# Norm tiles in the two banks of a PSUM pair declared independent of each other, reads by VectorE and ScalarE included

## The chip, the cores and the metric

The kernel runs on one core of a Trainium2 chip, in one launch. The metric is device time in microseconds (us), the median of three runs.

## The reference, cut to what matters

Two layers of a diffusion backbone run over 512 latent tokens (stream X) and 256 context tokens (stream C), model width 1024, in float32. Each sublayer is wrapped in two RMS norms ("sandwich"): the input of a sublayer is normed and modulated, its output is normed, scaled by a gate and added to the stream.

```
xm = rmsnorm(h, g_in) * (1 + scale) + shift          # "pre"
y  = sublayer(xm)                                     # SwiGLU, conv + Fourier mixer, or attention
h  = h + gate * rmsnorm(y, g_out)                     # "post"
```

The sublayers are SwiGLU, conv + Fourier mixer, SwiGLU in layer 0, and SwiGLU, attention, SwiGLU in layer 1. Five times a post of one sublayer is followed by the pre of the next, for each stream; the last post has no pre behind it.

## The kernel before, in words

Tokens lie along the free dimension and the 1024 features along 128 partitions in KT = 8 tiles. Every matrix product is done in three passes: operands are split in a high and a low part, and `mm3` (lines 209 to 216) issues `w_high x_high`, `w_high x_low`, `w_low x_high`. So each feature tile k of a normed input has a high part, made by ScalarE, and a low part, made by VectorE, and the second of three matmuls needs the low part.

`run` (line 107) walks a list of items, each some weight chunks and a function that issues the matmuls. Raw weights come in by SP's queue, ScalarE rounds them to `wh` (line 141), VectorE or GpSimd makes `wl` (line 143); while a norm is under way (`self.norms`) it is always GpSimd. Norms are generators that `advance` steps while matmuls are issued, by a clock that counts TensorE time; `yield 1.8` means that 1.8 us of matmuls are issued before the next piece. The framework then plans the order of each engine's queue from priorities and modelled durations, and puts in semaphore waits for the dependencies that it tracks on tiles.

A norm of one stream goes: `rnorm` (line 254) sums squares over partitions on TensorE (L261), makes a reciprocal root on VectorE (L279 to L288), and spreads it on TensorE (L267). Then `post` (line 319) does per tile k, all on VectorE unless said: a scaled `y` into PSUM scratch `t` (L331, "post norm"), the previous tile's addition of squares (L245), `h += t` (L335), and on ScalarE the square of `h` into `t` (L244). `pre` and `pre_tiles` (lines 291 to 318) do per tile: scaled `h` into scratch `t` (L311, "norm"), on ScalarE `x_high = t + B` (L313, "high"), and on VectorE `x_low = (t + B) - x_high` (L304, "low"). The order written is norm(k), high(k), low(k-1).

`scratch` (line 225) gives `t`. Streams of lane "c" (C, and B, the second half of the last sublayer) get a `mm` tile of their own, one bank, three in rotation. Streams of lane "x" (X with 512 columns, and A, the first half, with 256) get a half of a `pr` tile of 1024 columns, which spans two banks: even k the first half, odd k the second. In `pre` all eight tiles alternate in one `pr`; in `post` each pair k, k+1 takes a new `pr`, of two.

After the pre of X TensorE runs `lead4`, `lead6` or the latent projections: it goes through k = 0 to 7 with six matmuls of 512 columns (256 for A) per tile, and so consumes normed tiles as they come.

Of the kernel before, what the change touches and what calls it, by code (L numbers as in the profile page):

```python
# [10 lines left out]
F32 = mybir.dt.float32  # L11
# [3 lines left out]
AF = mybir.ActivationFunctionType  # L15
ALU = mybir.AluOpType
# [60 lines left out]
class Builder:  # L77
# [158 lines left out]
    def stats_add(self, s, st, src, sq, late=False):  # L236


        nc = self.nc
        if st.ssum is None:  # L240
            st.ssum = self.tmp.tile([P, s.n], F32, name=self.nm("ssum"), tag=f"ssum{s.lane}", bufs=1)
            nc.scalar.activation(out=st.ssum, in_=src, func=AF.Square)
        else:
            nc.scalar.activation(out=sq, in_=src, func=AF.Square)  # L244
            add = lambda: nc.vector.tensor_tensor(out=st.ssum, in0=st.ssum, in1=sq, op=ALU.add)  # L245
            if late:
                return add
            add()

    def new_stats(self):  # L250
# [47 lines left out]
    def pre_tiles(self, s, ks, A, B, rb):  # L298

        nc = self.nc  # L300
        done, last = [], None

        def low(k, x, t):
            nc.vector.scalar_tensor_tensor(out=x[:, 1], in0=t, scalar=B[:, k:k + 1], in1=x[:, 0].bitcast(F32),  # L304
                                           op0=ALU.add, op1=ALU.subtract)
            done.append((x[:, 0], x[:, 1]))

        for k in ks:
            x = self.xmpool.tile([P, 2, s.n], F32R, name=self.nm("xm"), tag=f"xm{s.name}{k}", bufs=1)
            t = self.scratch(s, k, True)  # L310
            nc.vector.scalar_tensor_tensor(out=t, in0=s.h[k], scalar=A[:, k:k + 1], in1=rb,  # L311
                                           op0=ALU.mult, op1=ALU.mult)
            nc.scalar.activation(out=x[:, 0], in_=t, func=AF.Identity, bias=B[:, k:k + 1])  # L313
            if last:
                low(*last)
            last = k, x, t
        low(*last)
        return done

    def post(self, s, st, A, want_stats=True):  # L320

        nc = self.nc
        y = s.y
        yield N1 if s.lane != "c" else N1C
        rb = yield from self.rnorm(s, st, D)
        new = self.new_stats()
        late = None
        for k in range(KT):
            with self.tc.high_priority(PRIORITY):
                t = self.scratch(s, k)  # L330
                nc.vector.scalar_tensor_tensor(out=t, in0=y[k], scalar=A[:, k:k + 1], in1=rb,  # L331
                                               op0=ALU.mult, op1=ALU.mult)
                if late:
                    late()
                nc.vector.tensor_tensor(out=s.h[k], in0=s.h[k], in1=t, op=ALU.add)  # L335
                if want_stats:
                    late = self.stats_add(s, new, s.h[k], t, True)
                    if k == KT - 1:
                        late()
            yield POST[0] if s.n == 512 else POST[1]  # L340
        yield 2.0
        return new
# [828 lines left out]
    def attend(self, gaps):  # L1171

        heads = [(g, kind, hd) for g in range(4) for kind, hd in HEADS]
        st, loads, wts = {}, {}, {}
        soft, avs, post, ends = [], [], [], []

        gap = 1.0
# [479 lines left out]
```

## Time and profile before

| | |
|---|---|
| runs | 2997.32, 2997.54, 2999.41 us; median 2997.54 |
| profiled execution | 2996.09 us, of which the span of instructions is 2994.3 us |
| mean granted TensorE clock | 0.988 |
| busy share of the span | TensorE 96%, VectorE 55%, ScalarE 35%, GpSimd 27% |
| DMA | 413 MB, mean 138 GB/s |

TensorE is busy nearly all the time, so what counts are the short stretches in which it waits, and the stretches in which its clock is granted at half. Busy shares of the other engines are averages over stages and tell little about such a stretch; the timelines of the stretch do. The five stretches in which a pre of lane "x" feeds TensorE begin at about 607, 850, 1431, 2010 and 2600 us of the span; they are called S1 to S5 here. S1 is the mixer's input, S2 and S3 the inputs of the two SwiGLUs behind it, S4 that of attention, S5 that of the last SwiGLU (stream A).

### The profile page before, as it was taken

The numbers are of one execution on the slowest core, as the hardware profiler recorded it, in microseconds if no ns is written. First come the engines' busy times: TensorE is split into PE (matmuls) and PEld (weight loads), VectorE is DVE, ScalarE is ACT, GpSimd is POOL, SyncE is SP. The second block draws the span as 40 slices with busy tenths as digits, with TensorE's granted clock in tenths as the row PEclk, the third lists the DMA queues.
The fourth block names the chain that finished last, engine by engine and source line by source line (L and its number), as shares of the span: only waits on it lengthen the run. The fifth ranks groups of instructions, "written<-read, shape, count | busy, mean of one in ns | idle before, by whom it ended". The sixth has DMA issues, their size and how long they took to land.

```text
span 2994.3 us, 44211 instructions
## 1 busy us (share of the span) xinstructions
PE 2874.3 (96%) x17842; PEld 2549.9 (85%) x17842; DVE 1650.9 (55%) x2966; ACT 1043.5 (35%) x1733; POOL 820.5 (27%) x441
## 2 busy tenths in 40 slices
PE   6999999999999999999999999999899999999998
PEld 5888888878878888888788888887788888899997
DVE  7866676565475433435845334366366667653335
ACT  4422121444343221124431122244344555552223
POOL 4221112423242111114311111143433332442222
PEclk9999999999999999999999999999999999999999
DMA  7754433323344322233333433352866685452334
GB/s 269 248 166 134 141 135 127 120 86 126 120 142 148 112 85 99 78 120 113 124 130 106 131 116 118 108 167 100 265 166 185 154 211 111 146 175 92 102 103 141
DMA packets 190095, 413.19 MB, mean 138 GB/s; under 512 B 58369, under 2 KB 83585, under 8 KB 189890
## 3 DMA queue, kind: packets, MB, share of 16 engines
q1 hardware_dynamic: 126930, 373.09, 37.6%
q0 software_dynamic: 62960, 37.27, 5.6%
q8 instruction: 140, 2.29, 0.3%
q14 instruction: 65, 0.53, 0.1%
HBM read 375.14 MB, written 35.00 MB: 137 GB/s over the span
## 4 chain that ended last, share of the span: by engine, by line
PE 63%; DVE 6%; DMA 3%; issue 2%; ACT 2%; POOL 2%; SPq 0%; ACTq 0%; POOLq 0%; DVEq 0%
PE mm L213 12%; PE mm L215 12%; PE mm L214 12%; PE pr L214 8%; PE pr L213 8%; PE pr L215 8%; PE pr L1021 2%; PE mm L1030 1%; ACT wh L141 1%; DVE wl L143 1%; DMA ks<-dr 1%; PE st L1115 1%; POOL wl L143 1%; DVE top L1011 1%; DMA dr<-stg 1%
## 5 line engine op out<-in xcount | busy, mean ns | idle before, releaser
L143 POOL TENSOR_TENSOR wl<-wraw,wh 128x1024 fp32r<-128x1024 f32 (+2 forms) x276 | 674.8, 2448 | 1898.1 <-ACT wh L141 1887.5
L141 ACT ACTIVATE wh<-wraw 128x1024 fp32r<-128x1024 f32 (+1 forms) x476 | 494.2, 1039 | 940.7 <-PE mm L214 577.8
L214 PE MATMUL pr<-xm,wh 128*128 128x512 f32 (+1 forms) x1760 | 635.5, 361 | 22.9 <-DVE xm L304 18.1
L213 PE MATMUL pr<-xm,wh 128*128 128x512 f32 (+1 forms) x1760 | 632.3, 360 | 8.3 <-DVE act L221 2.9
L215 PE MATMUL pr<-xm,wl 128*128 128x512 f32 (+1 forms) x1760 | 632.3, 359 | 0.0
L213 PE MATMUL mm<-xm,wh 128*128 128x256 f32 (+1 forms) x1560 | 460.1, 296 | 8.0 <-DVE xm L304 5.0
L215 PE MATMUL mm<-xm,wl 128*128 128x256 f32 (+1 forms) x1560 | 461.5, 296 | 1.8 <-DVE wl L143 1.8
L214 PE MATMUL mm<-xm,wh 128*128 128x256 f32 (+1 forms) x1560 | 460.4, 295 | 0.6 <-DVE xm L304 0.6
L213 PE MATMUL mm<-act,wh 128*128 128x256 f32 (+1 forms) x1408 | 454.1, 324 | 5.9 <-ACT y L504 2.1
L215 PE MATMUL mm<-act,wl 128*128 128x256 f32 (+1 forms) x1408 | 454.0, 323 | 2.6 <-POOL wl L143 2.6
L214 PE MATMUL mm<-act,wh 128*128 128x256 f32 (+1 forms) x1408 | 454.1, 323 | 1.5 <-DVE act L221 1.5
L214 PEld LDWEIGHTS pr<-xm,wh 128*128 128x128 f32 x1760 | 334.6, 190 | 83.5 <-DVE xm L304 27.0
L383 DVE CUSTOM_DVE_ANT_0 junk<-wmod,cond,bmod 128x1024 bf16<-128x1024 f32 x256 | 387.8, 1515 | 9.6 <-DMA wmod<-in_w_mod_dram 6.9
L213 PEld LDWEIGHTS pr<-xm,wh 128*128 128x128 f32 x1760 | 334.5, 190 | 61.4 <-DVE act L221 3.3
L215 PEld LDWEIGHTS pr<-xm,wl 128*128 128x128 f32 x1760 | 334.9, 190 | 51.2
L143 DVE TENSOR_TENSOR wl<-wraw,wh 128x1024 fp32r<-128x1024 f32 x200 | 251.5, 1257 | 210.0 <-ACT wh L141 209.5
L213 PEld LDWEIGHTS mm<-xm,wh 128*128 128x128 f32 x1560 | 295.7, 190 | 18.3 <-DVE xm L304 5.6
L215 PEld LDWEIGHTS mm<-xm,wl 128*128 128x128 f32 x1560 | 295.3, 189 | 10.2 <-DVE wl L143 2.4
L214 PEld LDWEIGHTS mm<-xm,wh 128*128 128x128 f32 x1560 | 295.3, 189 | 8.8 <-DVE xm L304 1.1
L213 PEld LDWEIGHTS mm<-act,wh 128*128 128x128 f32 x1408 | 265.3, 189 | 33.1 <-ACT act L220 3.6
L214 PEld LDWEIGHTS mm<-act,wh 128*128 128x128 f32 x1408 | 266.6, 189 | 26.2 <-DVE act L221 2.7
L215 PEld LDWEIGHTS mm<-act,wl 128*128 128x128 f32 x1408 | 265.8, 189 | 26.8 <-POOL wl L143 3.2
(240 smaller groups left out, 3445.7 us busy)
## 6 DMA issues: line engine op xcount, KB each, us to landing
wraw<-in_w_ffn_in_dram SPq DMA_DIRECT2D x250, 512.0 KB, 3.5
wmod<-in_w_mod_dram SPq DMA_DIRECT2D x160, 512.0 KB, 4.3
wraw<-in_w_ffn_out_dram SPq DMA_DIRECT2D x106, 512.0 KB, 3.6
dr<-stg SPq DMA_DIRECT2D x40, 512.0 KB, 4.7
wraw<-in_w_in_even_dram SPq DMA_DIRECT2D x32, 512.0 KB, 3.5
qs<-dr POOLq DMA_DIRECT2D x56, 256.0 KB, 11.7
dr<-stg SPq DMA_DIRECT2D x36, 256.0 KB, 6.7
ks<-dr POOLq DMA_DIRECT2D x24, 384.0 KB, 11.2
```

The source lines that it names most:

```text
L141: self.nc.scalar.activation(out=h, in_=r, func=AF.Copy)
L143: eng.tensor_tensor(out=l, in0=r, in1=h.bitcast(F32), op=ALU.subtract)
L213: mmul(out, w[0], x[0], start=first, stop=False)
L214: mmul(out, w[0], x[1], start=False, stop=False)
L215: mmul(out, w[1], x[0], start=False, stop=last)
L383: dot = nc.vector.tensor_tensor_reduce(out=junk, in0=w, in1=self.cond[n], op0=ALU.mult, op1=ALU.add, scale=1.0, scalar=self.bmod[:, l, row ...
L1011: nc.vector.tensor_reduce(top, ps, axis=AX.X, op=ALU.max, negate=True)
L1021: self.nc.tensor.matmul(ps[:, c0:c1], q, k[:, c0:c1], start=i == 0, stop=i == len(passes) - 1)
L1030: self.nc.tensor.transpose(ps[:, kt * P:(kt + 1) * P], w[:, (k0 + kt) * P:(k0 + kt + 1) * P], self.ident)
L1115: nc.tensor.matmul(ps, v[:, kt], wt[i][:, :, kt], start=kt == 0 and i == 0, stop=kt == 5 and i == 1)
```

## The change

The tiles' tracker treats accesses to one `pr` tile as dependent; the change declares certain pairs of instructions, which touch different halves, to be without dependency. In `pre_tiles`, for lane "x": norm(k+1) on high(k), and low(k) on high(k+1). In `post`, for lane "x" and odd k: post norm(k) on the square of k-1. `stats_add` returns the square's instruction for that. No instruction is added, removed or rewritten.

```diff
-            nc.scalar.activation(out=st.ssum, in_=src, func=AF.Square)
+            return nc.scalar.activation(out=st.ssum, in_=src, func=AF.Square), None
         else:
-            nc.scalar.activation(out=sq, in_=src, func=AF.Square)
+            square = nc.scalar.activation(out=sq, in_=src, func=AF.Square)
...
-                return add
+                return square, add
...
-        def low(k, x, t):
-            nc.vector.scalar_tensor_tensor(out=x[:, 1], in0=t, scalar=B[:, k:k + 1], in1=x[:, 0].bitcast(F32),
-                                           op0=ALU.add, op1=ALU.subtract)
+        def low(k, x, t, other=None):
+            ins = nc.vector.scalar_tensor_tensor(out=x[:, 1], in0=t, scalar=B[:, k:k + 1],
+                                                 in1=x[:, 0].bitcast(F32), op0=ALU.add, op1=ALU.subtract)
+            if other and s.lane != "c":
+                self.tc.declare_no_dep(ins.ins, other.ins, reason="another bank")
...
+            norm = nc.vector.scalar_tensor_tensor(out=t, in0=s.h[k], scalar=A[:, k:k + 1], in1=rb,
+                                                  op0=ALU.mult, op1=ALU.mult)
+            if last and s.lane != "c":
+                self.tc.declare_no_dep(norm.ins, high.ins, reason="another bank")
+            high = nc.scalar.activation(out=x[:, 0], in_=t, func=AF.Identity, bias=B[:, k:k + 1])
             if last:
-                low(*last)
+                low(*last, high)
...
+                norm = nc.vector.scalar_tensor_tensor(out=t, in0=y[k], scalar=A[:, k:k + 1], in1=rb,
+                                                      op0=ALU.mult, op1=ALU.mult)
+                if late and s.lane != "c" and k % 2:
+                    self.tc.declare_no_dep(norm.ins, square.ins, reason="another bank")
...
-                    late = self.stats_add(s, new, s.h[k], t, True)
+                    square, late = self.stats_add(s, new, s.h[k], t, True)
```

## Rows read from the trace of the kernel before

**Rows 1.** The page's first part: busy us, share of the span and instructions of each engine.

```profile
PE 2874.3 (96%) x17842; PEld 2549.9 (85%) x17842; DVE 1650.9 (55%) x2966; ACT 1043.5 (35%) x1733; POOL 820.5 (27%) x441
```

**Rows 2.** Who TensorE's matmuls waited for over the whole span: us in total, times, longest us.

```profile
PE pr L214 <- DVE xm L304: 18.1, 19, 2.1
PE mm L213 <- DVE xm L304: 5.0, 2, 4.6
```

**Rows 3.** Timeline of PE in S1, from the first matmul of the lead to the last of its seven waits for a low (tiles 0 to 6; the waits of tiles 0, 2 and 6 are shown): start us, us, engine, line, operation, tiles, count, and in brackets the idle time before and what ended it.

```profile
608.10 0.49 PE L213 MATMUL pr<-xm,wh 128*128 128x512 f32 x1
610.54 0.50 PE L214 MATMUL pr<-xm,wh 128*128 128x512 f32 x1 [1.94 <-DVE xm L304]
...
615.34 0.50 PE L214 MATMUL pr<-xm,wh 128*128 128x512 f32 x1 [0.64 <-DVE xm L304]
615.67 0.39 PE L215 MATMUL pr<-xm,wl 128*128 128x512 f32 x1
...
616.59 0.39 PE L213 MATMUL pr<-xm,wh 128*128 128x512 f32 x1
...
624.95 0.50 PE L214 MATMUL pr<-xm,wh 128*128 128x512 f32 x1 [0.60 <-DVE xm L304]
```

**Rows 4.** Timeline of DVE in S1, the norms (L311) and lows (L304) of stream X; columns as in rows 3.

```profile
608.08 0.76 DVE L311 SCALAR_TENSOR_TENSOR pr<-h,par,st 128x512 f32<-128x512 f32 x1
...
609.73 0.75 DVE L304 SCALAR_TENSOR_TENSOR xm<-pr,par,xm 128x512 fp32r<-128x512 f32 x1 [0.54 <-ACT xm L313]
...
613.02 0.76 DVE L311 SCALAR_TENSOR_TENSOR pr<-h,par,st 128x512 f32<-128x512 f32 x1
614.53 0.75 DVE L304 SCALAR_TENSOR_TENSOR xm<-pr,par,xm 128x512 fp32r<-128x512 f32 x1 [0.76 <-ACT xm L313]
615.32 0.76 DVE L311 SCALAR_TENSOR_TENSOR pr<-h,par,st 128x512 f32<-128x512 f32 x1
...
624.15 1.40 DVE L304 SCALAR_TENSOR_TENSOR xm<-pr,par,xm 128x512 fp32r<-128x512 f32 x2
```

**Rows 5.** Timeline of ACT in S1, the highs (L313) of tiles 0 and 3.

```profile
607.36 0.69 ACT L313 ACTIVATE xm<-pr,par 128x512 fp32r<-128x512 f32 x1 [1.68 <-DVE pr L311]
...
613.81 0.69 ACT L313 ACTIVATE xm<-pr,par 128x512 fp32r<-128x512 f32 x1 [1.61 <-DVE pr L311]
```

**Rows 6.** Timeline of DVE in two other pres, both with 256 columns: first stream C (a `mm` tile of its own for each k), then stream A (halves of one `pr`).

```profile
649.16 0.48 DVE L304 SCALAR_TENSOR_TENSOR xm<-mm,par,xm 128x256 fp32r<-128x256 f32 x1
...
649.95 0.48 DVE L304 SCALAR_TENSOR_TENSOR xm<-mm,par,xm 128x256 fp32r<-128x256 f32 x1
...
2605.07 0.49 DVE L311 SCALAR_TENSOR_TENSOR pr<-h,par,st 128x256 f32<-128x256 f32 x1
...
2606.62 0.49 DVE L311 SCALAR_TENSOR_TENSOR pr<-h,par,st 128x256 f32<-128x256 f32 x1
```

**Rows 7.** Timeline of PE in S2, its waits in the lead (tiles 3, 4 and 5).

```profile
862.16 0.50 PE L214 MATMUL pr<-xm,wh 128*128 128x512 f32 x1 [0.83 <-DVE xm L304]
...
864.90 0.50 PE L214 MATMUL pr<-xm,wh 128*128 128x512 f32 x1 [1.07 <-DVE xm L304]
...
868.70 0.50 PE L214 MATMUL pr<-xm,wh 128*128 128x512 f32 x1 [2.13 <-DVE xm L304]
```

**Rows 8.** Timeline of ACT in S2: two activations of the conditioning vectors (L365) and the high that stands behind the second of them.

```profile
862.43 1.06 ACT L365 ACTIVATE cond<-cond 128x1024 f32<-128x1024 f32 x1 [1.11 <-DMA cond<-in_c_dram]
...
866.23 1.06 ACT L365 ACTIVATE cond<-cond 128x1024 f32<-128x1024 f32 x1 [2.17 <-DMA cond<-in_c_ctx_dram]
867.19 0.67 ACT L313 ACTIVATE xm<-pr,par 128x512 fp32r<-128x512 f32 x1
```

**Rows 9.** Stretches by engine: stretch, its us, busy us (and instructions) of PE, PEld, DVE, ACT and POOL, granted TensorE clock, DMA share, GB/s. S1's lead whole, and a stretch of low clock in each of S2, S3 and S5.

```profile
608.00:627.50 19.50, 13.51 (x53) 9.02 (x53) 13.80 (x34) 6.97 (x12) 2.37 (x1) 1.00 0.14 51
...
869.50:876.20 6.70, 6.58 (x18) 4.84 (x17) 3.08 (x14) 1.43 (x2) 0.00 (x0) 0.50 0.01 2
1436.10:1442.80 6.70, 5.99 (x14) 4.46 (x14) 4.52 (x6) 1.87 (x4) 0.00 (x0) 0.50 0.23 78
...
2613.70:2617.00 3.30, 3.30 (x17) 3.30 (x16) 1.41 (x10) 1.82 (x2) 0.71 (x1) 0.50 0.00 0
```

**Rows 10.** Timeline of PE in S3, the first (tile 0) and the last (tile 6) of four waits in the lead.

```profile
1434.67 0.50 PE L214 MATMUL pr<-xm,wh 128*128 128x512 f32 x1 [1.90 <-DVE xm L304]
...
1449.08 0.50 PE L214 MATMUL pr<-xm,wh 128*128 128x512 f32 x1 [0.60 <-DVE xm L304]
```

**Rows 11.** Timeline of PE in S4: the last wait of the kind at the start of the lead, and a wait for stream C's first tile.

```profile
2014.02 0.50 PE L214 MATMUL mm<-xm,wh 128*128 128x512 f32 x1 [0.64 <-DVE xm L304]
...
2060.43 0.59 PE L213 MATMUL mm<-xm,wh 128*128 128x512 f32 x1 [4.58 <-DVE xm L304]
```

**Rows 12.** Timeline of PE in S5: the first wait (tile 0) and the last (tile 6).

```profile
2603.33 0.54 PE L214 MATMUL pr<-xm,wh 128*128 128x256 f32 x1 [1.79 <-DVE xm L304]
...
2613.40 0.39 PE L214 MATMUL pr<-xm,wh 128*128 128x256 f32 x1 [0.69 <-DVE xm L304]
```

**Rows 13.** Who VectorE's post norms waited for over the whole span: us in total, times, longest us.

```profile
DVE pr L331 <- ACT pr L244: 10.7, 4, 3.6
```

**Rows 14.** All instructions of `pre` of lane "c" on ACT and DVE: line, engine, operation, tiles, count, duration in ns (min/median/max), first and last start.

```profile
L313 ACT ACTIVATE xm<-mm,par x48: 455/473/477, 101.8 to 2645.9; 128x256 fp32r<-128x256 f32 x48
L304 DVE SCALAR_TENSOR_TENSOR xm<-mm,par,xm x48: 473/476/485, 102.4 to 2647.2; 128x256 fp32r<-128x256 f32 x48
```

More of the change, by code (lines that the diff above doesn't have):

```diff
@@ L310, in pre_tiles @@
             t = self.scratch(s, k, True)
-            nc.vector.scalar_tensor_tensor(out=t, in0=s.h[k], scalar=A[:, k:k + 1], in1=rb,
-                                           op0=ALU.mult, op1=ALU.mult)
-            nc.scalar.activation(out=x[:, 0], in_=t, func=AF.Identity, bias=B[:, k:k + 1])
+            norm = nc.vector.scalar_tensor_tensor(out=t, in0=s.h[k], scalar=A[:, k:k + 1], in1=rb,
[3 more added lines that the diff above has]
+            high = nc.scalar.activation(out=x[:, 0], in_=t, func=AF.Identity, bias=B[:, k:k + 1])
             if last:
-                low(*last)
+                low(*last, high)
             last = k, x, t
@@ L330, in post @@
                 t = self.scratch(s, k)
-                nc.vector.scalar_tensor_tensor(out=t, in0=y[k], scalar=A[:, k:k + 1], in1=rb,
-                                               op0=ALU.mult, op1=ALU.mult)
+                norm = nc.vector.scalar_tensor_tensor(out=t, in0=y[k], scalar=A[:, k:k + 1], in1=rb,
+                                                      op0=ALU.mult, op1=ALU.mult)
+                if late and s.lane != "c" and k % 2:
+                    self.tc.declare_no_dep(norm.ins, square.ins, reason="another bank")
                 if late:
```

## The prediction

> **What bounds the kernel now.** I read the page's busy shares first: TensorE is busy 96% of the span [rows 1], so a change that adds and removes no instruction can only gain where TensorE waits, or where its clock falls, and it can only lose by making it wait. The view of who waited for whom, for TensorE, then says which of its waits the change can reach: 23.1 us for a low part (L304), the largest item [rows 2]. The timelines of the stretches with those waits came next: TensorE's for how long, VectorE's and ScalarE's for why.
>
> In S1 TensorE starts the lead at 608.10, stops at the first matmul that needs a low, and stops again in each of the tiles 0 to 6; from tile 0's to tile 6's low-part matmul are 624.95 - 610.54 = 14.41 us, 2.40 a tile [rows 3]. Unhindered, four matmuls take 616.59 - 615.67 = 0.92 us, so a tile's six take 1.38 [rows 3]. The missing microsecond is VectorE's pace: norm to norm 615.32 - 613.02 = 2.30 us [rows 4]. In those 2.30 us it works twice 0.75 and idles 0.76, until a high is done. That high is the wrong one: low(2) starts at 614.53, and ScalarE's high of tile 3, in the other half of the tile, ended at 613.81 + 0.69 = 614.50 [rows 4, 5]. So norm(k+1), high(k+1), low(k) run one after another though low(k) needs only high(k). The first tile shows the same: high(0) ended at 608.05, norm(1) began at 608.08, low(0) only at 609.73 [rows 4, 5]. The control is in the same trace: stream C, with a tile per k, makes a 256-column tile every 649.95 - 649.16 = 0.79 us, stream A, with halves of one tile, every 2606.62 - 2605.07 = 1.55 [rows 6].
>
> **The change, part by part.** It takes away waits, issues nothing, and moves no DMA; no wait is added. The one indirect effect is that the planner may order VectorE's and ScalarE's queues otherwise, since tiles come sooner in its model.
>
> The new pace: a norm straight behind a low takes 615.32 - 614.53 = 0.79 us, a low behind an unrelated norm as much as one low behind another, 1.40 - 0.75 = 0.65 [rows 4]. Together 1.45 a tile instead of 2.30, nearly TensorE's 1.38. ScalarE's 0.69 per tile [rows 5] fits beside it. What is late next is VectorE itself, by 0.07 a tile.
>
> *S1.* Six tiles at 1.45 take 8.7 instead of 14.41: 5.7 gained. Low(0) can follow norm(1) at 608.08 + 0.65, 1.0 sooner than 609.73; I take 0.8. VectorE's other work, that ran in its idle time (leftovers of stream C's sums, C's reciprocal root), is now on the path: I estimate two long instructions at 0.65 [rows 4], 1.3. Sum **5.2**; ends 3.5 (twice as much comes between, and the first tile gains less) and 6.5 (nothing comes between).
>
> *S3.* From tile 0 to tile 6 again 14.41 us [rows 10], but 6.7 us of them at half the clock [rows 9]: matmuls were slow instead of waiting. Full gain as in S1, 5.2. If the clock falls at the same place, 6.7 us at half are 3.35 us of work lost, and the gain is near 2. S1, with the same first wait, 1.94 against 1.90, kept its full clock [rows 3, 9, 10], and a shorter wait is no reason to fall. I take **4.5**, ends 2 and 6.5.
>
> *S2.* Waits of 0.83 + 1.07 + 2.13 = 4.03 [rows 7], then 6.7 us at half clock, 3.35 [rows 9]: 7.4 at most. Here highs stand in ScalarE's queue behind the two activations of conditioning vectors, which wait for a DMA until 862.43 and 866.23 [rows 8]; the change doesn't hasten those. With tiles at 1.45 the planner should place most highs ahead of them. If the second stays ahead of high(6), low(6) ends near 867.19 + 0.67 + 0.75 = 868.6, where TensorE could be at 862.16 - 0.83 + 3 x 1.38 = 865.5: 3.1 lost, and perhaps the clock again. **6.0**, nearer the free end because low(3) to low(5) no longer wait for the next high; ends 1 and 7.4.
>
> *S5.* Tile 0 to tile 6 take 2613.40 - 2603.33 = 10.07 us [rows 12]; at stream C's 0.79 [rows 6] 4.7. That is 5.3, with 0.8 of the first wait of 1.79, less 0.6 for other work: **5.5**; ends 4.0, and 7.2 if the 3.3 us at half clock behind it [rows 9] go as well.
>
> *S4.* Only the start waits for a low, 0.64 [rows 11]; later TensorE has other matmuls to fill in. What is gained may be waited for at 2060, where TensorE stands 4.58 us for stream C's first tile [rows 11]. **0.5**, ends 0 and 0.9.
>
> *Post.* Four of VectorE's post norms wait 10.7 us for a square [rows 13]. That wait stays nearly whole: the addition behind needs the same square, so only one norm of 0.75 goes ahead of it. TensorE has stream C's work meanwhile. **0.5** for all, ends 0 and 1.2.
>
> *Given back.* Stream C's pres are unchanged, and TensorE comes to them sooner. They start from TensorE's own norm matmuls, which come sooner too, so I estimate a loss of only **1.2**, from the 4.58 of rows 11; ends 0 and 3.
>
> Sum 5.2 + 4.5 + 6.0 + 5.5 + 0.5 + 0.5 - 1.2 = **21.0 us**; all best ends give 29.7, all worst 7.5. The profiled execution took 2996.09 us (span 2994.3 and 1.8 around it), 1.45 under the median of the runs shown: 2996.1 - 21.0 = 2975.1, which in runs like the median is **2976.5**.
>
> **Rivals.** *The clock falls all the same.* S2, S3 and S5 show a clock at half behind waits of 0.6 to 2.1 us, S1 does not with the same waits [rows 3, 7, 9, 10]; what decides the level is not seen here. If S2, S3 and the end of S5 keep their slow stretches, with S2's second activation in the way, the gains are S1 5.2, S2 1, S3 2, S5 4.5, others -0.2: 12.5 us, **2985**. A rule bears on this: the Trainium skill, "TensorE: Matmul & The Clock Gate", section "A second HAM failure mode: psum-queue depth-cycling", tells of a kernel whose many short idles between groups of matmuls made the clock swing between its two levels. By that rule a lead that still waits a little in each tile keeps its slow stretches; S1, seven waits at a clock of 1.00 [rows 3, 9], speaks against it.
>
> *Nothing changes.* If low(k) is held by another dependency on the same `pr` tile than the declared pair, the waits stay: **2997.5**. Against it: the instruction that ends 0.03 us before each low is exactly the declared one [rows 4, 5].
>
> *Slower.* VectorE and ScalarE would now work on the two halves of a `pr` at the same time, which they hardly do before. If that slows both, the tile costs a norm and a low at the longer duration; past 2.30 / 2 = 1.15 us an instruction (now 0.75) the pre is slower than before. At 1.4 us a tile takes 2.8, 0.5 more than now: 8 tiles in five leads, 20 us, **3017**. Against it: lane "c" has highs beside norms and lows in separate tiles, and durations there keep to 455 to 477 ns and 473 to 485 ns over 48 of each [rows 14]. The Trainium skill, "PSUM — Partial Sum Buffer", section "Specifications (TRN2)", has it that both engines keep full bandwidth in parallel unless they meet in one bank; rows 14 agree.
>
> **How the numbers follow.** Chances: forecast 0.66, the clock rival 0.22, nothing 0.07, slower 0.05. A measurement of this kernel tells 0.2%, 6 us, from no change. Forecast and clock rival are both faster by more than that except at their worst ends, so faster 0.87, same 0.08, slower 0.05. The range runs from all best ends together, 2997.5 - 29.7 = 2967.8, to all worst ends together, 2997.5 - 7.5 = 2990, and so holds the clock rival. It leaves out the last two cases, 0.12, and a little of the first two for a new order of the queues.
>
> **What would show it.** In the changed profile, norms and lows of stream X should alternate on VectorE about every 0.7 us without idle time before L304; TensorE's waits for a low should drop from 23.1 us to 10 or less, nearly half of it the 4.6 of stream C; the distance of tile 0 to tile 6 should be 9 to 10 us in S1 and S3 and about 5 in S5; the half-clock stretches at S2 and S3 should be gone or shorter. I am wrong if L304 still starts when the next high ends; if L311, L304 or L313 take longer than 0.76 us; or if the pres run at the new pace and the span does not follow, which would mean that TensorE waits the same time later on, first of all for stream C.

## The result, and the profile after

The changed kernel took 2971.78 us, the median of four executions (2964.97 to 2975.79), the kernel before beside it 2997.43 (2996.24 to 2999.41): a ratio of 0.9916, 95% interval 0.9899 to 0.9932, 25 us less. Measured again in a later group of runs it was 0.9924 (0.9910 to 0.9938), 2975.59 us against 2995.37. The prediction was 2976.5. The profiled execution of after took 2964.97 us, 6.8 under its median, so its 31 us less than the profile of before are more than the change is worth; the profile of the second measurement (2974.29 us) stands beside it below.

The first part of the page of after, to set against [rows 1]:

```profile
PE 2860.0 (97%) x17842; PEld 2539.2 (86%) x17842; DVE 1646.8 (56%) x2966; ACT 1042.0 (35%) x1733; POOL 820.2 (28%) x441
```

The counts are those of before. Whom TensorE waited for (us in total, times, longest us), against [rows 2]:

```profile
PE st L261 <- DVE ssum L245: 12.9, 6, 6.7
...
PE mm L213 <- DVE xm L304: 6.8, 4, 5.3
...
PE pr L214 <- DVE xm L304: 1.5, 5, 0.4
```

The wait for a low inside a lead fell from 18.1 to 1.5 us. The other one, at a tile's first matmul, grew from 5.0 to 6.8, and 5.3 of that is stream C's first tile in S4. Now S1. TensorE: the lead's first matmul, the low matmuls of tiles 0 to 2, and that of tile 6 (against [rows 3]):

```profile
606.58 0.49 PE L213 MATMUL pr<-xm,wh 128*128 128x512 f32 x1
607.50 0.50 PE L214 MATMUL pr<-xm,wh 128*128 128x512 f32 x1 [0.42 <-DVE xm L304]
...
609.14 0.50 PE L214 MATMUL pr<-xm,wh 128*128 128x512 f32 x1
...
610.79 0.51 PE L214 MATMUL pr<-xm,wh 128*128 128x512 f32 x1
...
617.44 0.39 PE L214 MATMUL pr<-xm,wh 128*128 128x512 f32 x1
```

VectorE in the same stretch (norms are now L313, lows still L304), against [rows 4]:

```profile
608.34 0.74 DVE L304 SCALAR_TENSOR_TENSOR xm<-pr,par,xm 128x512 fp32r<-128x512 f32 x1
609.00 0.41 DVE L245 TENSOR_TENSOR ssum<-ssum,mm 128x256 f32<-128x256 f32 x1
609.33 0.75 DVE L313 SCALAR_TENSOR_TENSOR pr<-h,par,st 128x512 f32<-128x512 f32 x1
609.99 0.75 DVE L304 SCALAR_TENSOR_TENSOR xm<-pr,par,xm 128x512 fp32r<-128x512 f32 x1
610.65 0.41 DVE L512 TENSOR_TENSOR y<-y,mm 128x256 f32<-128x256 f32 x1
610.98 0.75 DVE L313 SCALAR_TENSOR_TENSOR pr<-h,par,st 128x512 f32<-128x512 f32 x1
```

And ScalarE, the highs (now L317) of tiles 1 to 3, against [rows 5]:

```profile
607.50 0.67 ACT L317 ACTIVATE xm<-pr,par 128x512 fp32r<-128x512 f32 x1
608.07 0.38 ACT L244 ACTIVATE mm<-y 128x256 f32<-128x256 f32 x1
608.47 0.69 ACT L317 ACTIVATE xm<-pr,par 128x512 fp32r<-128x512 f32 x1
610.12 0.69 ACT L317 ACTIVATE xm<-pr,par 128x512 fp32r<-128x512 f32 x1 [0.96 <-DVE pr L313]
```

Low(1) starts at 608.34, while high(2) only starts at 608.47: a low no longer waits for the next tile's high. VectorE has hardly any idle time left, and each of the tiles 0 to 4 takes 1.65 us: a norm 0.66, a low 0.66, and 0.33 for a 256-column addition of stream C that it does in between. TensorE follows at the same 1.65. The same stretch by engine (busy us and instructions of PE, PEld, DVE, ACT, POOL, then granted clock, DMA share, GB/s), against the first row of [rows 9]:

```profile
608.00:616.90 8.90, 8.89 (x38) 6.08 (x37) 8.77 (x17) 4.90 (x9) 2.07 (x1) 1.00 0.27 92
```

VectorE is busy 8.77 of 8.90 us, where it was 13.80 of 19.50. The waits of S3 (tile 0, then tile 6) and S5 (the same two), against [rows 10, 12]:

```profile
1420.73 0.50 PE L214 MATMUL pr<-xm,wh 128*128 128x512 f32 x1 [0.42 <-DVE xm L304]
...
1430.65 0.40 PE L214 MATMUL pr<-xm,wh 128*128 128x512 f32 x1
...
2578.96 0.39 PE L214 MATMUL pr<-xm,wh 128*128 128x256 f32 x1 [0.22 <-DVE xm L304]
...
2584.69 0.28 PE L214 MATMUL pr<-xm,wh 128*128 128x256 f32 x1
```

From tile 0 to tile 6 it is 9.94 us in S1, 9.92 in S3, 5.73 in S5, where it was 14.41, 14.41 and 10.07. In S2 (against [rows 7, 8]) ScalarE's two activations now stand before the last high only, and one wait is left:

```profile
856.23 1.06 ACT L371 ACTIVATE cond<-cond 128x1024 f32<-128x1024 f32 x1 [2.53 <-DMA cond<-in_c_dram]
858.35 1.06 ACT L371 ACTIVATE cond<-cond 128x1024 f32<-128x1024 f32 x1 [1.05 <-DMA cond<-in_c_ctx_dram]
859.31 0.67 ACT L317 ACTIVATE xm<-pr,par 128x512 fp32r<-128x512 f32 x1
860.01 0.75 DVE L304 SCALAR_TENSOR_TENSOR xm<-pr,par,xm 128x512 fp32r<-128x512 f32 x1 [3.18 <-ACT xm L317]
861.24 0.58 PE L261 MATMUL st<-ones,ssum 128*128 128x1 f32 x4 [2.05 <-DVE ssum L245]
```

In S4 (against [rows 11]) VectorE's wait in stream C's post grew from 2.32 us to 7.40, and TensorE's for C's first tile from 4.58 to 5.28. The first line is of before, the other two of after:

```profile
2033.62 0.49 DVE L331 SCALAR_TENSOR_TENSOR mm<-y,par,st 128x256 f32<-128x256 f32 x1 [2.32 <-ACT ssum L242]
...
2014.85 0.49 DVE L335 SCALAR_TENSOR_TENSOR mm<-y,par,st 128x256 f32<-128x256 f32 x1 [7.40 <-ACT ssum L242]
...
2041.54 0.79 PE L213 MATMUL mm<-xm,wh 128*128 128x512 f32 x1 [5.28 <-DVE xm L304]
```

In the post (against [rows 13]) no norm waits for a square any more; the addition behind it does, which shows in VectorE's waits as 12.4 us where it had been 5.4 (before, then after):

```profile
DVE ssum L245 <- ACT pr L244: 5.4, 10, 1.0
...
DVE ssum L245 <- ACT pr L244: 12.4, 13, 2.5
```

**Where the time went**, from the starts of the matmuls: both kernels issue 17842, and the i-th of one is set against the i-th of the other. The table gives by how much a kernel fell back against the profile of before in a stretch (stretches by the times of before, us; minus means that it gained). Stretches between those listed are left out. "Again" is the second execution of after; the last two columns are kernels without the declarations for the pre (experiments below), and show what differs by chance between two executions.

| stretch | after | again | pre only | post only | old, conditioning later |
|---|---|---|---|---|---|
| to 590 | 2.1 | 1.5 | 1.7 | 0.2 | 0.9 |
| 590 to 660, S1 | -9.7 | -9.8 | -9.2 | -3.9 | -3.1 |
| 660 to 910, S2 | -4.7 | -6.7 | -2.7 | 1.1 | 2.0 |
| 1425 to 1480, S3 | -5.9 | -5.0 | -6.0 | 0.2 | 0.1 |
| 2005 to 2030, S4 | -1.0 | -1.1 | -0.4 | 1.4 | -2.0 |
| 2030 to 2110, behind S4 | 4.2 | 2.5 | -1.8 | -0.5 | -0.8 |
| 2450 to 2500, attention | -4.8 | 0.7 | -0.8 | -2.9 | -0.9 |
| 2595 to 2625, S5 | -7.2 | -7.3 | -7.1 | -1.7 | -1.6 |
| all | -31.3 | -21.9 | -26.3 | -5.1 | -5.7 |

In S1 and S5 the kernels without the change gain 3.1 to 3.9 and 1.6 to 1.7 as well. The profile of before has half-clock stretches there, at 596.4 to 603.2 and 2613.6 to 2617.0 us, in which TensorE was busy throughout (6.80 of 6.80 and 3.40 of 3.40 us); half their length is 3.4 and 1.7. Less what the last two columns show, the change gives about 6 in S1, 5 to 6 in S3, 5.5 in S5 and 6 to 9 in S2 (it varies most), and from 2005 to 2110 the two executions of after lose 1 to 3. That is some 20 to 23 us.

The attention row is chance. In windows of the two executions of the same changed program, first the one of 2964.97 us, then the one of 2974.29 (columns as in the window above):

```profile
2440.00:2465.00 25.00, 20.45 (x138) 17.83 (x136) 18.00 (x40) 13.83 (x33) 5.71 (x6) 1.00 0.91 174
```

```profile
2440.00:2465.00 25.00, 18.76 (x98) 16.01 (x97) 11.25 (x29) 11.45 (x25) 5.72 (x6) 0.82 1.05 191
```

The granted clock is 1.00 in one and 0.82 in the other, and of the 9.3 us between the two, 5.5 arise there in the table. Before had such a stretch too.

### The profile page after: what moved, and what is told of

The parts are those of the page before. It is cut to its first block, busy times and chain, and to the rows that moved or that the text cites. A ratio compares the mean times of both kernels' runs of the same rounds, so it can differ in the third digit from the quotient of the medians.

```text
span 2963.2 us, 44211 instructions
## 1 busy us (share of the span) xinstructions
PE 2860.0 (97%) x17842; PEld 2539.2 (86%) x17842; DVE 1646.8 (56%) x2966; ACT 1042.0 (35%) x1733; POOL 820.2 (28%) x441
## 5 line engine op out<-in xcount | busy, mean ns | idle before, releaser
L213 PEld LDWEIGHTS mm<-xm,wh 128*128 128x128 f32 x1560 | 295.4, 189 | 18.9 <-DVE xm L304 6.1
## 6 DMA issues: line engine op xcount, KB each, us to landing
ks<-dr POOLq DMA_DIRECT2D x24, 384.0 KB, 10.8
```

Source lines behind the costliest of these rows:

```text
L213: mmul(out, w[0], x[0], start=first, stop=False)
```

## The experiments

All times are medians, ratios are to the kernel before on the same chip, with 95% intervals. The kernel before ranged over 2988 to 3006, 2987 to 3012 and 2986 to 3007 us in the three groups of runs.

**Which declaration it is.** Four kernels take the change apart. The first leaves out the declaration in `post`:

```diff
-                if late and s.lane != "c" and k % 2:
-                    self.tc.declare_no_dep(norm.ins, square.ins, reason="another bank")
```

> Only the two declarations in pre_tiles, none in post. My theory: the whole gain is in the pre, so about 2972 (25 us under the kernel before), tile 0 to tile 6 in S1 and S3 near 10 us. Rival 'post': the shorter post brings a share of its own, then 2977 or more. Rival 'planner': the time comes from a new order of queues, then anything between 2965 and 2997 without relation to the tile pace.

Measured: 2971.88 us, ratio 0.9909 (0.9876 to 0.9941), the whole gain. VectorE's post norm waits 10.8 us for a square, as in the kernel before. (A pace, here and below, is the mean distance between the starts of the eight lows of a pre.)

The second leaves out the two in `pre_tiles` and keeps that of the post:

```diff
-            if other and s.lane != "c":
-                self.tc.declare_no_dep(ins.ins, other.ins, reason="another bank")
...
-            if last and s.lane != "c":
-                self.tc.declare_no_dep(norm.ins, high.ins, reason="another bank")
```

> Only the declaration in post. My theory: 2996 to 2998, the wait for the square moves from the post norm (L331) to the addition behind it, tile 0 to tile 6 in S1 stays at 14.4 us. Rival 'post': 2991 or less. Rival 'planner': off 2997 by several us either way.

Measured: 2993.23 us, ratio 0.9986 (0.9973 to 0.9999), 3 us under the expected range. The lows keep their old distance in S3 (2.16 us on average, 2.15 in before), TensorE waits 20.6 us for them, and the post norms' wait has moved to the additions:

```profile
DVE ssum L245 <- ACT pr L244: 12.3, 14, 2.4
```

So the declaration in the post is worth 4 us (0.14%) or, by the interval's end, nothing: it moves a wait by one instruction. Against pre only, the whole change gains nothing by it.

The other two have none in the post and one of the pre's each: the first `if` of the diff just shown, low(k) on high(k+1), then the second, norm(k+1) on high(k).

> Only low(k) on high(k+1) is declared independent; norm(k+1) still waits for high(k). My theory: norm(k+1) starts at 0.75 + 0.69 = 1.44 us after norm(k), which is the pace that VectorE allows anyway (1.45), so nearly the whole gain: 2972 to 2976. Rival: the two waits are worth alike, then about 2985.

Measured: 2976.56 us, ratio 0.9921 (0.9895 to 0.9948), 22 of the 27 us that both declarations of the pre gave on the same chip. In S3, VectorE:

```profile
1422.14 0.76 DVE L313 SCALAR_TENSOR_TENSOR pr<-h,par,st 128x512 f32<-128x512 f32 x1
1422.80 0.75 DVE L304 SCALAR_TENSOR_TENSOR xm<-pr,par,xm 128x512 fp32r<-128x512 f32 x1
1423.46 0.41 DVE L508 TENSOR_TENSOR y<-y,mm 128x256 f32<-128x256 f32 x1
1423.79 0.75 DVE L313 SCALAR_TENSOR_TENSOR pr<-h,par,st 128x512 f32<-128x512 f32 x1
```

The tile takes 1.65 us here too: with stream C's addition in the gap, norm(k+1) comes no earlier than high(k) ends anyway. Where nothing stands in the gap it waits, so the lows of S3 are 1.72 us apart on average, against 1.49 with both.

> Only norm(k+1) on high(k) is declared independent; low(k) still waits for high(k+1). My theory: the chain norm, high, low keeps its 2.30 us a tile and only the first tile can start sooner, 2994 to 2998. Rival: the two waits are worth alike, then about 2985.

Measured: 2993.42 us, ratio 0.9981 (0.9964 to 0.9997), just under the expected range and hardly told from no change. VectorE in S3:

```profile
1441.03 0.75 DVE L311 SCALAR_TENSOR_TENSOR pr<-h,par,st 128x512 f32<-128x512 f32 x1
1442.54 0.75 DVE L304 SCALAR_TENSOR_TENSOR xm<-pr,par,xm 128x512 fp32r<-128x512 f32 x1 [0.76 <-ACT xm L315]
1443.33 0.76 DVE L311 SCALAR_TENSOR_TENSOR pr<-h,par,st 128x512 f32<-128x512 f32 x1
```

Norm to norm is 2.30 again: the low waits for the next high, and the next norm stands behind the low in VectorE's queue. The declaration that brings most of the gain is low(k) on high(k+1), as [rows 4, 5] had said. A new order of the queues, the rival named in three of the expectations, is not what acts in S1: up to low(4) norms and lows follow one another on VectorE in the same order in before and after.

**The same pace by other means.** The kernel before, with tiles of their own instead of halves:

```diff
-            t = self.scratch(s, k, True)
+            t = self.mm()[:, :s.n]
```

> The kernel before without any declaration; in pre, streams X and A take a mm tile of their own for each k, as stream C does, instead of halves of a pr tile. My theory (the wait is one of bookkeeping on a shared tile): lows of S1 and S3 come every 1.5 us as with the change, 2972 to 2978; up to 5 us may be lost because mm tiles are shared with stream C's matmuls. Rival 'planner' (the declarations act through a new order of queues): the pace stays at 2.15 or the time does not follow it.

Measured: 2999.1 us, ratio 1.0009 (0.9988 to 1.0031). The pace came without any declaration, 1.25 us a tile in S1 to S4 where 1.5 had been expected, quicker than after's; the time did not. VectorE in S3:

```profile
1437.69 0.74 DVE L311 SCALAR_TENSOR_TENSOR mm<-h,par,st 128x512 f32<-128x512 f32 x1
1438.35 0.74 DVE L304 SCALAR_TENSOR_TENSOR xm<-mm,par,xm 128x512 fp32r<-128x512 f32 x1
1439.01 0.74 DVE L311 SCALAR_TENSOR_TENSOR mm<-h,par,st 128x512 f32<-128x512 f32 x1
```

The same `mm` tiles serve stream C's matmuls, and the pre now takes them away. Against before TensorE gains 3.2 us in S3 and 4.4 in S5 (stretches as in the table; 1.6 to 1.7 of the latter come without any change), but loses 5.0 in S2 and 9.9 at S4. TensorE, in S2 and before S4's lead:

```profile
858.83 0.58 PE L213 MATMUL mm<-a,wh 128*128 128x256 f32 x1 [5.85 <-DVE xm L304]
...
2019.67 0.58 PE L213 MATMUL mm<-act,wh 128*128 128x256 f32 x1 [9.07 <-DVE xm L304]
```

So a quicker pre is not enough; the declaration gives it without taking a tile from anyone. The expectation had allowed 5 us for this loss, and it was larger: that is what this miss taught.

**What is left in S2.** The conditioning vectors' load and activation are put at the start of the work that is spread over the next sublayer, first in the old kernel, then in the changed one:

```diff
-            b.adaln_open(names, spread)
-            if work:
-                b.spread(work, FFN_US)
+            if not work:
+                b.adaln_open(names, spread)
+            else:
+                b.spread([lambda: b.adaln_open(names, spread)] + work, FFN_US)
```

> The kernel before, with the load and activation of the conditioning vectors (L365) made the first piece of the spread work, so behind the norms, not ahead of them. My theory on S2: its waits of tiles 4 and 5 (1.07 and 2.13 us) and the slow stretch come from those activations in ScalarE's queue; without them S2 waits about 0.65 in each tile as S1 does: 2994 to 2998, a gain of 0 to 3 us. Rival: the activations set S2's waits alone, then S2 loses its 4.0 us of waits and the time is 2990.

> The changed kernel with the same move. My theory: in the changed kernel the activations stand ahead of high(7) and of stream C's square, and TensorE waits 2.05 us for C's sums in S2; that wait goes: 2 us less than the changed kernel, 2968 to 2972. Rival: the wait moves elsewhere (the loads then collide with the modulation weights), no difference, 2972.

Measured: 2997.71 us, ratio 1.0003 (0.9982 to 1.0024), and 2972.15 us, ratio 0.9906 (0.9869 to 0.9943). Neither tells anything about S2, because the edit did not do what it should: the planner put both activations back among the highs (855.03 and 857.27 us in the second, high(7) behind them), and the waits stayed (0.85, 1.25 and 2.40 us in the first). So both were run again with the activations also kept in the order in which they are written:

```diff
-                nc.scalar.activation(out=t, in_=src, func=AF.Silu)
+                silu = nc.scalar.activation(out=t, in_=src, func=AF.Silu)
+                self.tc.keep_in_program_order(silu)
```

> The changed kernel, and the two activations of conditioning vectors kept in the order in which they are written, behind both norms of S2 instead of ahead of the last high. Theory (they are what holds low(7) and TensorE's sum of squares behind it by 2 us): low(7) follows its norm without the 3.2 us of idle time, the pace of S2 falls from 2.15 to about 1.5 to 1.7 us a tile, TensorE's wait of 2.05 us for C's sum goes, and the time is 1 to 3 us lower than the changed kernel's, which a measurement hardly tells. Rival (something else of ScalarE's or VectorE's queue holds it): pace of S2 stays above 1.9.

Measured: 2974.79 us, ratio 0.9919 (0.9903 to 0.9935). The lows of S2 are 1.65 us apart (2.15 in after), low(7) follows without a wait, TensorE's wait of 2.05 us is gone, and TensorE gains 2.5 us over after between 835 and 910 us. The total shows none of it: the edit moves the first pair of activations too, and against after TensorE has lost 5 us by 590, most of it between 105 and 130.

> The kernel before, with only the move of e12: the two activations behind both norms of S2, no declaration. Theory (in S2 two causes hold TensorE, the wrong high and the activations' DMA): the pace of S2 falls from 2.68 to the 2.15 of S1 and S3, waits of TensorE for lows of about 0.6 a tile remain, and the time falls by 1 to 5 us, 2992 to 2996; if the 6.8 us at half clock behind them go too, by the upper end. Rival (the activations alone cause S2's loss): S2's waits for lows vanish without any declaration.

Measured: 2995.48 us, ratio 0.9999 (0.9986 to 1.0012). TensorE in S2:

```profile
869.00 0.50 PE L214 MATMUL pr<-xm,wh 128*128 128x512 f32 x1 [0.84 <-DVE xm L304]
871.30 0.50 PE L214 MATMUL pr<-xm,wh 128*128 128x512 f32 x1 [0.63 <-DVE xm L304]
873.59 0.51 PE L214 MATMUL pr<-xm,wh 128*128 128x512 f32 x1 [0.63 <-DVE xm L304]
```

Without the activations S2 looks like S1 and S3 of before: a tile every 2.30 us and 0.6 of waiting in each. Two causes held S2, as the theory had it; the pace came out at 2.32 on average, not 2.15. The time did not fall by the expected 1 to 5 us: TensorE gains 2.9 between 660 and 910, but has fallen 8.6 behind before by 590, where the first pair of activations moved as well.

**What S4 gives back.** The query latents sum into three `mm` tiles at once, so that stream C's post finds none. Two of the three sums go into the halves of a `pr` tile, first on top of the edit of S2 that did nothing, then alone:

```diff
-            pss = [self.mm()[:, :SEQ] for _ in range(3)]
+            pair = self.pr()
+            pss = [pair[:, :SEQ], pair[:, 512:512 + SEQ], self.mm()[:, :SEQ]]
```

> The kernel of e7, and at S4 the query latents accumulate in one pr tile (two halves) and one mm tile instead of all three mm tiles, so that stream C's post has scratch. My theory: VectorE's wait of 7.4 us before C's post at S4 goes, and with it TensorE's 5.3 us for C's first tile: 4 to 5 us less than e7, 2964 to 2968. Rival: the missing pr tile holds back the query projections by as much, no difference or slower.

Measured: ratio 0.9882 (0.9836 to 0.9928), from 2962.23, 2963.52 and 2973.73 us; a fourth execution took 9509.53 us and is not in it, and no profile shows why.

> The changed kernel with one more edit: the three accumulators of the query latents take the two halves of one pr tile and one mm tile, where they took all three mm tiles. Theory (what S4 gained is given back because stream C's pre needs mm tiles, and the query latents hold all three of them until ScalarE has emptied them): the post of C no longer waits 7.4 us for an mm tile, C's first tile is ready earlier, TensorE's wait of 5.3 us near 2040 us goes, and 3 to 5 us of time with it: 2966 to 2969 beside 2971 for the changed kernel in the same job. Rival (TensorE then waits as long a little later, for C's later tiles or for attention's inputs): the wait near 2040 goes but the time stays that of the changed kernel, within 2 us.

Measured: 2968.52 us, ratio 0.9907 (0.9887 to 0.9926), beside 2975.59 and 0.9924 (0.9910 to 0.9938) for the unaltered changed kernel on the same chip:

> The changed kernel unaltered, once more, for a direct comparison and for the spread of its single executions. Theory: ratio to the kernel before 0.991, so 2969 to 2974, and in its profile the same paces of the lows (1.47, 2.15, 1.49, 1.37 and 0.90 us a tile in S1 to S5, within 0.05), since these follow from the order of the queues; only the stretches at half clock lie elsewhere and have another sum than 39.7 us. Rival (the paces too vary from execution to execution): they differ by more than 0.1.

In the latents' kernel VectorE's wait of 7.40 us and TensorE's of 5.28 are gone, and TensorE gains 4.7 us between 2030 and 2056 of before. Then it waits for C's sum and loses 4.0 by 2110, at half clock:

```profile
2053.37 0.35 PE L261 MATMUL st<-ones,ssum 128*128 128x1 f32 x2 [2.74 <-DVE ssum L245]
```

```profile
2054.00:2061.00 7.00, 7.00 (x35) 7.00 (x36) 1.90 (x12) 2.46 (x5) 4.82 (x3) 0.52 0.42 153
```

Where the 5.28 come from is shown: the three `mm` tiles. What the edit is worth is not: the medians are 7 us apart, but the intervals overlap, and the profiled execution is one without the slow stretch in attention. The unaltered kernel confirms the paces in S1, S3, S4 and S5 within 0.01 us a tile (1.47, 1.49, 1.37, 0.90), but not in S2 (1.80 against 2.15), where high(7) waits for a DMA; there the expectation missed, and its time of 2975.59 us lies a little over the expected 2969 to 2974.

## Why the prediction was right

*The mechanism* held: the low waits for the wrong high, and the declaration of that pair brings most of the gain (experiments with one declaration each). Durations did not change, so the rival "slower" (contention for the two halves) is refuted. From the costliest groups by line of after (instructions, total us, mean ns, idle us before); in before the three had 753, 748 and 684 ns:

```profile
L313 DVE SCALAR_TENSOR_TENSOR pr<-h,par,st 128x512 f32<-128x512 f32 x32 | 23.1, 751 | 0.0
L304 DVE SCALAR_TENSOR_TENSOR xm<-pr,par,xm 128x512 fp32r<-128x512 f32 x32 | 23.4, 748 | 3.5 <-ACT xm L317 3.2
L317 ACT ACTIVATE xm<-pr,par 128x512 fp32r<-128x512 f32 x32 | 21.8, 685 | 18.7 <-DVE pr L313 18.6
```

The Trainium skill, "PSUM — Partial Sum Buffer", section "Specifications (TRN2)", says that the two engines keep full bandwidth unless they meet in one bank; these rows agree.

*S1*: 5.2 predicted, 6.0 by the rows. Tile 0 to 6 gave 14.41 - 9.94 = 4.5, as the 5.7 less 1.3 for other work had it; the first wait fell by 1.94 - 0.42 = 1.5, not 0.8. That was the under-sized part: I let low(0) follow a norm(1) that still waited for high(0), but the second declaration takes that wait away too, and norm(1) now starts at 605.71, before high(0) does (605.83). *S3*: 4.5 predicted, 4.49 + 1.48 = 6.0 by the rows. The stretch at half clock that I allowed for did not cost anything: post only, without that stretch, is level with before in S3 (0.2 in the table), because VectorE set the pace there either way. *S5*: 5.5 predicted, 5.5 found in the table less chance, 4.34 + 1.57 = 5.9 by the rows. *S2*: 6.0 predicted, 4.7 and 6.7 in the two executions, 6 to 9 less what the kernels without the change lose there. The planner did put most highs ahead of the activations, as assumed, and only the last high stayed behind them; the tile they delay is 7, not 6. *Post*: 0.5 predicted, not told from nothing; the wait moved to the addition, as the text had it.

*S4*: 0.5 predicted, 1.0 found in the table.

*Given back*: 1.2 predicted, with an end of 3. The size was near: TensorE stands 20.4 us ahead of before at 2030 (times of before) and 18.9 when C's first tile is there, in the second execution 19.2 and 17.8, so some 1.5 is given back at that wait. The reason given for it failed, that C's pres "start from TensorE's own norm matmuls, which come sooner too". In S4 stream C's post has to wait for an `mm` tile until ScalarE has emptied the query latents; it starts 18.8 us sooner (2033.62 and 2014.85), and C's first tile comes with it. With only the pre's declarations the pre of S4 is slower (1.90 us a tile) and the wait for C shorter (3.42), and TensorE stands 19.0 us ahead at the same place: hurrying that pre has no use. A further 2.9 and 1.0 us are lost between 2075 and 2110. There after has half-clock stretches of 3.4 us (by its own times at 2061.8 and 2089.1, in the second execution at 2087.4) and before has none; the prediction had no term for this, and what of it belongs to the change is open.

*The sum*: the stretches give 20 to 23 us against 21.0. S1 and S3 gave more than predicted and the clock behind S4 took some back, so that the total comes this near is in part luck.

*The clock rival* fell, though not as a question of the clock: the waits that it needed are gone, and S1, S2, S3 and S5 have a granted clock of 1.00 from their first to their last tile. What remains are stretches at half clock in other places: up to the last matmul 28.2 us in one execution of after and 46.1 in the other, 64.0 in before (the 39.7 of the expectation above counts the end of the program, behind the last matmul, too). They lie near the start, ahead of S2 (829.6), behind S4 and in attention, and as the windows of attention show they differ between executions of one program. Over all profiles of this study they sum to 51.3 to 67.9 us in the kernels without the declaration of the lows and to 28.2 to 51.2 in those with it, so part of the gain may be clock. The means are 61.0 and 44.6; at half their length, 16 us less of them would be worth 8 at most, an estimate. As a slow stretch costs nothing where another engine sets the pace (S3), how much of it is not settled.

*Nothing changes* is refuted: the waits for a low inside a lead fell from 18.1 to 1.5 us.

## What to carry to other kernels

When an instruction starts a few hundredths of a microsecond after one whose result it does not use, look at how the framework tracks the tile they share: halves of one tile count as one object, and a pipeline over three engines falls into a row. Find the one pair that closes the loop; of three declarations here one brought most of it (22 of 27 us). Ask of a tile freed or taken who else rotates through the same buffers: own tiles for the pre gave a better pace (1.25 against 1.49) and no time at all.

## What the runs showed of the hardware

VectorE starts an instruction that needs nothing of its neighbour 0.65 to 0.66 us after the one before, though that one is recorded as 0.75 long (608.34 to 609.00). A norm that overwrites what the low just ahead of it reads came 0.79 after it [rows 4]. With a tile of its own, in the experiment with own tiles, a norm came 0.66 after the low ahead of it (1438.35 to 1439.01). So in this pair the dependency on the instruction just ahead costs 0.13 us even inside one engine, and in after an addition of stream C between the two fills that time.
